# Input loads moved from ACT's DMA queue into SP's queue, between the output stores, in a batched q·kᵀ kernel on Trainium2

## Chip, cores, metric

One core of one Trainium2 chip. The metric is the device time of one execution in microseconds (us), lower is better. A run is called slow when it is over 1.5% above the fastest of the same kernel, and fast otherwise. The profile is one execution, and all profile times count from the start of its span. It calls TensorE's matmuls PE and its weight loads PEld, VectorE DVE, ScalarE ACT, GpSimd POOL and SyncE SP. The granted clock is the share of TensorE's full clock that the profile records as allowed. A transfer lands when the profile has all of it as arrived.

## The reference

```python
# q, k: float32 [8, 12, 1024, 64]
np.einsum('bhid,bhjd->bhij', q, k).astype(np.float32)   # [8, 12, 1024, 1024]
```

Each of the 96 heads reads 0.5 MB and writes 4.19 MB. In all, 50 MB are read and 403 MB written.

## The kernel before

Heads are worked on in blocks: sizes G = 1, 1, 2, then 4, and a block has 2·G heads. I number heads from 0 throughout: blocks 0 and 1 hold heads 0 to 3, block 2 heads 4 to 7, block 3 heads 8 to 15, and so on by eights. A block's input comes in four loads (q and k of its first G heads, then q and k of its second G heads), goes through a float32 buffer (three of them; blocks 0 to 2 use the space of the first output buffer instead), is cast to float16 on POOL (GpSimd), transposed on PE during the first heads of the block before, and then multiplied. Four output buffers of 4 MB each are filled by ACT and DVE from PSUM and stored by SP.

```python
    in_pool = ctx.enter_context(tc.tile_pool(name="in_pool", bufs=3))
    half_pool = ctx.enter_context(tc.tile_pool(name="half_pool", bufs=1))
    out_pool = ctx.enter_context(tc.tile_pool(name="out_pool", bufs=4))
    ...
        def scores(self, n, side):            # one head
            ...
            for t in range(NT):               # 8 row tiles
                ...two matmuls, one copy to o_sb on DVE or ACT...
                if t in side:
                    side[t]()                 # transposes for the next block, after t = 1 and t = 6
            pin(nc.sync.dma_start(out=of[self.first + n]..., in_=o_sb...))
    ...
    def refill(i):                            # b: block i, c: block i + 1
        if b:
            ...
            for n in range(3):
                b.cast(n)
        yield
        if b:
            b.load(3, nc.scalar)
            b.cast(3)
        if c:
            c.load(0, nc.scalar)
            c.load(1, nc.scalar)
        yield
        yield
        if c:
            c.load(2, nc.scalar)
    ...
            b.scores(n, side)
            for job in todo:
                next(job, None)
            if nxt and n == nxt.G - 1 and i > 0:
                todo.append(refill(i + 2))
                next(todo[-1])
                if n == 2 * b.G - 1:
                    next(todo[-1])
```

So a refill spreads its four loads over several heads, and a load can only be issued once the cast of the piece that had its buffer is done.

Of the kernel before, what the change touches and what calls it, by code (L numbers as in the profile page):

```python
# [15 lines left out]
def kernel(  # L16
# [6 lines left out]
    nc = tc.nc  # L23
# [141 lines left out]



    def refill(i):
        b = blocks[i] if i < len(blocks) else None
        c = blocks[i + 1] if i + 1 < len(blocks) else None  # L170
        if b:
            half_sb = half_pool.tile([P, 2 * half_elems], F16, tag="half")
            b.place(half_sb, 0)
            for n in range(3):
                b.cast(n)
        yield
        if b:
            b.load(3, nc.scalar)
            b.cast(3)
        if c:  # L180
            c.load(0, nc.scalar)
            c.load(1, nc.scalar)
        yield
        yield
        if c:
            c.load(2, nc.scalar)

    blocks[0].alloc()
    for x in range(2):
# [1 line left out]
    todo = []  # L191
    for i, b in enumerate(blocks):
        nxt = blocks[i + 1] if i + 1 < len(blocks) else None
        if nxt:
            nxt.alloc()
        for n in range(2 * b.G):
            side = {}
            if nxt and n < nxt.G:
                side = {
                    1: lambda: nxt.transpose(n, 0),  # L200
                    6: lambda: nxt.transpose(n, 1),
# [4 lines that stand above are left out]
            if nxt and n == nxt.G - 1 and i > 0:  # L206
                todo.append(refill(i + 2))
                next(todo[-1])
                if n == 2 * b.G - 1:
                    next(todo[-1])  # L210


# [28 lines left out]
```

## Time and profile before

| | before |
|---|---|
| time, median of 3 | 1070.81 us (1069.8 to 1071.56) |
| bytes moved by DMA | 453.40 MB, 424 GB/s over the span |
| busy share of the span | PE 70%, DVE 47%, ACT 45%, POOL 9% |
| chain that ended last | 70% stores, 12% matmuls, 5% loads |

In the page's slices a DMA digit of 9 means that the 16 DMA engines were at least 90% busy. When every slice but the last has a 9, no compute engine sets the time, whatever its own share. The prediction shows these lines and reads them.

### The profile page before, as it was taken

How to read it: one execution, taken by the hardware profiler on the slowest of the kernel's cores; microseconds unless marked ns; L12 is line 12 of the kernel's file. 1: busy time of each engine (PE TensorE's matmuls, PEld its weight loads, DVE VectorE, ACT ScalarE, POOL GpSimd, SP SyncE). 2: the span in 40 equal slices, each digit the busy share in tenths (PEclk: the TensorE clock that was granted, in tenths of full speed). 3: DMA queues.
4: the chain of work that ended last, by engine and by line, in shares of the span. 5: the costliest groups of instructions: out<-in, count | busy, mean ns of one | idle time of the engine just before them, and what ended most of it. 6: DMA issues, size and time to landing. Idle time of an engine off the chain costs nothing.

```text
span 1069.1 us, 6245 instructions
## 1 busy us (share of the span) xinstructions
PE 752.0 (70%) x2304; PEld 270.0 (25%) x2304; DVE 506.9 (47%) x384; ACT 476.3 (45%) x481; POOL 91.6 (9%) x62
## 2 busy tenths in 40 slices
PE   7774976775785786677587678668668769767740
PEld 2231322321221232232122223223123223222210
DVE  4664743542652563354265356337336537433420
ACT  4442553453444444344345445435444545544530
POOL 3202020020020020002002002000100200000000
PEclk9765555555555555555555555555555555555555
DMA  9999999999999999999999999999999999999996
GB/s 391 419 407 426 433 429 433 427 429 433 429 432 430 432 432 424 437 428 432 429 429 425 431 432 430 421 436 431 424 425 434 429 432 431 432 432 433 431 431 265
DMA packets 21920, 453.40 MB, mean 424 GB/s; under 512 B 2432, under 2 KB 2432, under 8 KB 3968
## 3 DMA queue, kind: packets, MB, share of 16 engines
q1 hardware_dynamic: 14976, 406.85, 88.8%
q10 hardware_dynamic: 6912, 46.14, 10.4%
q8 instruction: 18, 0.29, 0.1%
q14 instruction: 14, 0.11, 0.0%
HBM read 50.33 MB, written 402.65 MB: 424 GB/s over the span
## 4 chain that ended last, share of the span: by engine, by line
DMA 76%; PE 15%; ACT 4%; POOL 1%; DVE 1%; issue 0%; ACTq 0%; SPq 0%; POOLq 0%
DMA out_dram<-o_sb 70%; PE ps L128 12%; ACT o_sb L132 4%; DMA x_sb<-in_k_dram 3%; DMA x_sb<-in_q_dram 2%; PE t_ps L103 2%; POOL half_sb L88 1%; DVE o_sb L130 0%; DMA early<-in_q_dram 0%; DVE qT L115 0%; DVE kT L115 0%; ACTq L132 0%; SPq L75 0%; POOLq L88 0%; SPq L136 0%
## 5 line engine op out<-in xcount | busy, mean ns | idle before, releaser
L128 PE MATMUL ps<-kT,qT 64*128 64x512 f16 x1536 | 666.5, 618 | 253.3 <-ACT o_sb L132 226.9
L132 ACT COPY o_sb<-ps 128x1024 f32<-128x1024 f32 x480 | 475.0, 1013 | 551.5 <-DMA out_dram<-o_sb 310.7
L130 DVE COPY o_sb<-ps 128x1024 f32<-128x1024 f32 x288 | 353.1, 1227 | 498.4 <-DMA out_dram<-o_sb 364.7
L128 PEld LDWEIGHTS <-qT 64*128 64x128 f16 x1536 | 196.9, 135 | 657.2 <-issue 649.8
L88 POOL CAST half_sb<-x_sb 128x2048 f16<-128x2048 f32 x44 | 82.2, 1893 | 766.7 <-PE t_ps L103 547.7
L103 PE MATMUL t_ps<-ident,half_sb 128*128 128x128 f16 x768 | 97.8, 307 | 29.3 <-POOL half_sb L88 29.3
L115 DVE COPY qT<-t_ps 128x1024 f16<-128x1024 f16 x48 | 110.6, 2304 | 13.7 <-PE t_ps L103 13.7
L103 PEld LDWEIGHTS <-half_sb 128*128 128x128 f16 x768 | 73.1, 140 | 106.5 <-issue 73.6
L115 DVE COPY kT<-t_ps 128x1024 f16<-128x1024 f16 x48 | 58.3, 1215 | 16.0 <-PE t_ps L103 16.0
L88 POOL CAST half_sb<-early 128x512 f16<-128x512 f32 (+1 forms) x12 | 8.7, 755 | 5.6 <-DMA early<-in_q_dram 5.3
L132 ACT ACT_TABLE_LOAD x1 | 1.3, 1283 | 7.8 <-DMA early<-in_q_dram 7.8
masks.py:199 POOL TENSOR_SCALAR_AFFINE_SELECT ident<-ident 128x128 f16<-128x128 f16 x1 | 0.3, 292 | 0.1
masks.py:197 POOL MEMSET ident<- 128x128 f16 x1 | 0.2, 204 | 0.3 <-POOLq L225 0.3
L225 POOL MEMSET const-float32-0.0<- 128x1 f32 x1 | 0.1, 98 | 0.2 <-issue 0.2
L225 POOL MEMSET const-bfloat16-1.0<- 128x1 bf16 x1 | 0.1, 101 | 0.0
L225 POOL MEMSET const-uint8-127<- 128x1 uint8 x1 | 0.1, 101 | 0.0
L225 POOL MEMSET const-float32-1.0<- 128x1 f32 x1 | 0.1, 98 | 0.0
## 6 DMA issues: line engine op xcount, KB each, us to landing
out_dram<-o_sb SPq DMA_DIRECT2D x96, 4096.0 KB, 34.1
x_sb<-in_k_dram ACTq DMA_DIRECT2D x22, 1024.0 KB, 18.7
x_sb<-in_q_dram ACTq DMA_DIRECT2D x20, 1024.0 KB, 29.6
x_sb<-in_q_dram SPq DMA_DIRECT2D x2, 1024.0 KB, 11.5
early<-in_q_dram SPq DMA_DIRECT2D x4, 256.0 KB, 5.0
early<-in_k_dram ACTq DMA_DIRECT2D x4, 256.0 KB, 5.2
early<-in_q_dram SPq DMA_DIRECT2D x2, 512.0 KB, 7.4
early<-in_k_dram ACTq DMA_DIRECT2D x2, 512.0 KB, 8.0
```

What stands on the lines that cost most here:

```text
L88: nc.gpsimd.tensor_copy(out=self.halves[n % 2][:, :, n // 2], in_=self.raw[n].rearrange("p (r d) -> p r d", d=D),)
L103: pin(nc.tensor.transpose(t_ps[:, t], rows, ident))
L115: pin(nc.vector.tensor_copy(out=dst, in_=src))
L128: pin(nc.tensor.matmul(ps[:, js], qT[cs, g, t], kT[cs, g, js]))
L130: pin(nc.vector.tensor_copy(out=o_sb[:, t], in_=ps))
L132: pin(nc.scalar.copy(out=o_sb[:, t], in_=ps))
L225: nc = _bacc.Bacc("TRN2", target_bir_lowering=False, num_devices=1)
```

## The change

Its intent: keep all later traffic on one queue, in an order that the program fixes, and take the DMA issues off ACT, which also copies results. The loads go to `nc.sync`, at slightly other places between the stores.

```diff
-        yield
-        if b:
-            b.load(3, nc.scalar)
+            b.load(3, nc.sync)
             b.cast(3)
         if c:
-            c.load(0, nc.scalar)
-            c.load(1, nc.scalar)
-        yield
+            c.load(0, nc.sync)
         yield
         if c:
-            c.load(2, nc.scalar)
+            c.load(1, nc.sync)
+        yield
+        yield
+        yield
+        if c:
+            c.load(2, nc.sync)
...
                 todo.append(refill(i + 2))
                 next(todo[-1])
-                if n == 2 * b.G - 1:
-                    next(todo[-1])
```

## The prediction

> **What bounds the kernel now.** I read the page's slices, queues and issue table first, then busy time by stretches of time, then the issue times on SP's and ACT's queues, and last the chain that ended last over its first 175 us. The page:
>
> ```profile
> DMA  9999999999999999999999999999999999999996
> GB/s 391 419 407 426 433 429 433 427 429 433 429 432 430 432 432 424 437 428 432 429 429 425 431 432 430 421 436 431 424 425 434 429 432 431 432 432 433 431 431 265
> ...
> q1 hardware_dynamic: 14976, 406.85, 88.8%
> q10 hardware_dynamic: 6912, 46.14, 10.4%
> ...
> out_dram<-o_sb SPq DMA_DIRECT2D x96, 4096.0 KB, 34.1
> x_sb<-in_k_dram ACTq DMA_DIRECT2D x22, 1024.0 KB, 18.7
> x_sb<-in_q_dram ACTq DMA_DIRECT2D x20, 1024.0 KB, 29.6
> ```
>
> The DMA engines are full from the first slice to the last but one, and SP's queue (q1) alone takes 88.8% of them. PE is busy 70% of the span and no other engine over 47%. So bytes bound the kernel: 453.40 MB at 430 GB/s are 1054 us of the 1069.1 us span, and the rest is start and end. The stretches say what loads beside stores cost (columns: stretch, its length, busy us of PE, PEld, DVE, ACT, POOL, granted clock, DMA share, GB/s):
>
> ```profile
> 58.10:63.20 5.10, 3.11 (x14) 1.49 (x14) 1.22 (x1) 1.07 (x2) 1.89 (x1) 0.50 0.94 386
> 63.20:70.00 6.80, 6.80 (x28) 2.86 (x26) 5.61 (x4) 3.79 (x4) 0.00 (x0) 0.50 1.00 366
> 85.60:107.50 21.90, 10.38 (x36) 4.00 (x36) 7.42 (x6) 4.99 (x6) 4.70 (x3) 0.50 1.01 432
> 110.00:862.00 752.00, 547.30 (x1657) 195.89 (x1656) 367.49 (x276) 341.00 (x344) 65.32 (x35) 0.50 1.00 430
> 882.00:1042.00 160.00, 115.39 (x306) 38.87 (x305) 71.71 (x56) 79.14 (x80) 0.00 (x0) 0.50 1.00 432
> ```
>
> From 110 to 862 us loads run beside stores at 430 GB/s; from 882 to 1042 us there are stores only, at 432. There is nothing to win in the steady part but 0.5%. What can move the time is an interval in which the DMA engines have nothing queued. Only the start comes near that; its chain:
>
> ```profile
> 41.53 16.56 DMA x_sb<-in_k_dram
> 58.09 0.05 issue
> 58.14 1.90 POOL half_sb L88
> 60.05 0.05 issue
> 60.09 1.03 PE t_ps L103 x8
> ...
> 84.71 17.71 DMA x_sb<-in_k_dram
> 102.42 0.05 issue
> 102.47 1.90 POOL half_sb L88
> 104.38 0.05 issue
> 104.42 1.03 PE t_ps L103 x8
> ```
>
> Twice PE waits for the cast of a late load, finishes the head with it, and SP issues that head's store at 63.16 and 107.50 us: 5.07 and 5.08 us after the load landed. While PE waited, the queue lived on earlier stores.
>
> **What the Trainium skill says.** Page "DMA: Bandwidth & Descriptors", section "Where 436 GB/s comes from", puts the ceiling of the 16 ports at 435.2 GB/s; the store-only stretch at 432 agrees. (The same section has HBM's side bind at about 358; this trace does not show that.) Section "Issuing engines are not separate DMA queues" says that DMAs from any issuer run on the same 16 engines and interleave, so that a second issuer saves only issue time; 430 against 432 agrees. Section "Queues, rings and completion order" says that an engine takes turns between queues packet by packet and takes one queue's descriptors in order. The trace agrees: a store row is 32 KB and a load row 8 KB (mean packets 27 and 6.7 KB), so in turns loads get about 8/40 of 430 GB/s, 12.2 us for 1 MB (estimate), and the landings at 90.3, 102.4 and 139.2 us lie 12.1 and three times 12.3 us apart. Page "DMA: Bandwidth & Descriptors", section "Anatomy of one DMA", says that any wait on a semaphore happens on the issuing sequencer before dispatch; SP's row of waits (848.4 us of the span in front of stores) agrees.
>
> **The change part by part.** I number heads from 0. The built program keeps the order of PE, DVE and POOL; ACT loses its 41 later loads, and SP issues them between stores.
>
> Removed: 41 issues on ACT at 0.34 us, 14 us beside 45% of busy time. ACT is not the bound: zero. Also removed: the turn-taking that lets a load pass the stores in front of it.
>
> Moved: the third load of each refill (the q piece of the second half) is now issued after the fourth further store, one head later in the steady part, where it used to go after the third. In the one short block (heads 4 to 7) it moves from behind head 5 (71.17 us before) to behind head 7.
>
> Added: a load waits on SP for its raw buffer, that is for a cast, and the stores behind it wait too.
>
> Steady part. A store takes 4.19 MB / 430 = 9.75 us, a load 2.44 us, so a block of eight stores and four loads takes 87.8 us. A head is made in about 7 us without transposes (16 matmuls x 0.43 us) and 9 us with them. Four output buffers let about three stores wait behind the one that runs; the median landing of 34.1 us says 3.5 stores. The waits of SP in front of loads are two or three casts of 1.89 us after the transposes, some 2 to 6 us, against a cushion of at least three stores less the making of one head, 29 - 9 = 20 us. A load issued behind a store lands within some 35 us, and its cast is needed four or more heads later. So nothing runs dry: zero per block, eleven blocks.
>
> First gap, head 4. The k load that head 4's second transpose needs is issued at 41.5 us, as before, but directly behind store 3 (issued 41.52). By 41.5 us 24.1 MB were issued (7.34 of loads, four stores) and 403 x 41.5 = 16.7 MB moved, so 7.4 MB or 17.2 us are left; the load lands at about 41.5 + 17.2 + 2.4 = 61.1, plus up to 1 us, against 58.1. Store 4 comes 5.07 us after that, at about 66.5. Behind the load only one more load is queued, 2.44 us. Issue to first byte is about 1.3 us (first issue at 0.74 us, first bytes at about 2). The gap is 5.07 - 2.44 + 1.3 = 3.9 us. The kernel before lost something here too: from 41.5 to 70 us it moved about 1.0 MB less than at 432, 2.3 us. If that goes away, the net is +1.6; if not, +3.9. I take +2.5.
>
> Second gap, head 8. Its first transposes (after row tile 1) need the third load of the block, now issued behind store 7. Heads 5 to 7 follow store 4 by 22.4 us (63.16 to 85.58 before), so that store 7 and the load are issued at about 89. Everything older runs first: from about 68 us four stores and one load, 41.4 us, then it, landing at about 112 instead of 90.3. PE stands still until its cast is done, 1.94 us later. From there the trace before has 92.22 to 97.7 for transposes and row tiles 2 to 6 (5.5 us), and then 3.1 us from the second transposes to the store's issue: together 10.5 us from landing to store 8. Meanwhile the queue holds only two loads, 4.9 us. The gap is 10.5 - 4.9 + 1.3 = 6.9 us, and some 0.4 us for the load's landing after its last byte: 7.3 us. It does not depend on when the load lands. Before, the DMA engines lost nothing here (432 GB/s from 85.6 to 107.5).
>
> After it. Stores 9 to 11 follow at 9 to 10.3 us, transposes included, against 9.75 us a store plus one load between: margins of about 3 us, tight but dry nowhere. From head 12 on 7 us a head fill the queue again.
>
> Sum: 1070.8 + 2.5 + 7.3 = 1080.6. Every idle microsecond of the bound adds to the end, as nothing later catches up with it. I say **1080.5 us**, 0.9% longer.
>
> **The rivals.**
> - The loads are hidden anyway (same time, 1071): the bytes are the same, and the early waits might be covered by the backlog. For it: 430 GB/s at every place after 110 us. Against: the backlog behind the late load, 4.9 us, is shorter than the 10.5 us that the next store needs.
> - One queue is served better (1064 to 1068): without turn-taking the engines don't switch between 32 KB stores and 8 KB loads. For it: a queue's time per MB, 10.4% x 1069.1 / 46.14 = 2.41 us for loads against 2.33 for stores, and 366 to 386 GB/s near 60 us. Against: 3% of 46 MB are 3 us at most, and the early small loads explain part. Even 435 GB/s throughout would save only some 12 us, so faster by over 2% (21 us) is out of reach.
> - Waits at SP's head empty the queue in every block (1100 and more): 3 us in eleven blocks would be 33 us. For it: a load's buffer waits for a cast that waits for another load in the same queue. Against: that older load is then behind at most one or two stores, and one more store stands behind it. I find the cushion of 15 to 20 us hard to use up, but this is the only way to slower by over 2%.
>
> **Range and chances.** The second gap is firm within 2 us, the first within 3; the turn-taking may give back up to 3, and a third gap at heads 9 to 11 may add up to 4. That makes 1074 to 1088. Faster 0.01, same 0.93, slower 0.06.
>
> **What would show it.** Right: SP's queue alone carries about 450 MB; loads land later than the 18.7 and 29.6 us of before, in the thirties; throughput falls well below 400 GB/s near 64 us and near 120 us, and is 430 from 160 us on; store 8 is issued about 10.5 us after the late q load landed, at about 122; the shift of late stores against before is the sum of the two gaps and then constant. Wrong: stores shifted by less than 4 us at 200 us; or a shift that grows from block to block (the third rival); or a steady rate that differs from 430 by more than 2 GB/s.

## The result

The changed kernel takes **1090.26 us** (median of 4, 1087.41 to 1090.55) against 1071.18 us (median of 4, 1069.80 to 1072.11) for the kernel before. The ratio is 1.0173, 95% interval 1.0153 to 1.0194. Ratios here are the mean time of one kernel's fast runs over that of the other's of the same rounds, so not quite the ratio of the medians. It is inside 2%, but 19 us longer where the prediction had 10, and outside its range of 1074 to 1088.

The page of the changed kernel: the slices, the stores' queue, and the issues with their median time to landing (last column, us).

```profile
DMA  9989799999999999999999999999999999999994
GB/s 385 423 316 424 302 394 422 439 430 423 430 433 424 432 432 427 429 425 434 424 429 435 429 433 430 425 438 428 428 434 428 435 427 437 429 436 430 437 427 212
...
q1 hardware_dynamic: 20880, 449.85, 96.8%
...
out_dram<-o_sb SPq DMA_DIRECT2D x96, 4096.0 KB, 34.3
x_sb<-in_q_dram SPq DMA_DIRECT2D x22, 1024.0 KB, 37.5
x_sb<-in_k_dram SPq DMA_DIRECT2D x21, 1024.0 KB, 36.0
```

Slices 3 and 5 (54 to 82 us and 109 to 136 us) have fallen to 316 and 302 GB/s; a full engine set gives 430. From slice 7 on the row looks like the one of before. The loads now land after some 36 to 38 us instead of 19 to 30. The same in stretches, first the kernel before and then the changed one (columns as in the prediction; the last two are DMA share and GB/s):

```profile
41.50:70.00 28.50, 16.78 (x62) 6.70 (x60) 12.95 (x9) 8.81 (x9) 5.57 (x3) 0.50 0.99 397
110.00:140.00 30.00, 29.76 (x100) 11.17 (x99) 23.10 (x17) 17.68 (x19) 4.45 (x3) 0.50 1.01 431
```

```profile
41.50:70.00 28.50, 11.16 (x38) 3.96 (x35) 8.30 (x6) 6.31 (x7) 7.15 (x4) 1.00 0.81 335
110.00:140.00 30.00, 19.20 (x73) 7.99 (x74) 14.07 (x10) 9.73 (x10) 3.79 (x2) 1.00 0.71 292
200.00:880.00 680.00, 485.93 (x1474) 173.81 (x1473) 326.43 (x246) 302.98 (x306) 57.88 (x31) 1.00 1.00 430
```

From 200 to 880 us both kernels move 430 GB/s, and from 880 to 1040 us both 432. So the loss is made before 200 us. In time at 430 GB/s it is (397 - 335) x 28.5 / 430 = 4.1 us in the first stretch, (431 - 292) x 30 / 430 = 9.7 us in the second, and by the same working 1.8 us from 70 to 110 us (430 against 411 GB/s) and 1.2 us from 140 to 200 us (432 against 423): 16.8 us. The spans differ by 1088.8 - 1069.1 = 19.7 us; the other 3 us lie after 1040 us, where the queue drains. The chain of the changed kernel names the waits:

```profile
43.52 21.09 DMA x_sb<-in_k_dram
64.61 0.05 issue
64.67 1.91 POOL half_sb L88
...
96.64 21.90 DMA x_sb<-in_q_dram
118.55 0.05 issue
```

The first is the load that head 4 needs, issued right behind store 3; the second is the load that head 8 needs, issued right behind store 7. The timeline has the stores that depend on them at 69.69 us (5.08 after the landing) and 128.97 us (10.42 after it). Before, the same stores were issued at 63.16 and 107.50 us. The second gap in steps of 2 us:

```profile
122.00:124.00 2.00, 2.00 (x6) 0.66 (x5) 2.00 (x1) 1.41 (x2) 0.98 (x1) 1.00 0.03 12
124.00:126.00 2.00, 2.00 (x7) 0.55 (x6) 1.29 (x2) 1.37 (x2) 0.00 (x0) 1.00 0.00 0
```

PE and DVE are busy with head 8, and the DMA engines have nothing at all to move. The engines do not stop together: from 120 to 122 us the share is still 0.60, and a share of 0.03 of 16 engines over the next 2 us is one engine for 1 us. So the last of the sixteen stops 1 to 2 us after most of the others.

### The profile page after: what moved, and what is told of

Its sections match the earlier page's. It is cut to its first block, busy times and chain, and to the rows that moved or that the text cites. A ratio compares the mean times of both kernels' runs of the same rounds, so it can differ in the third digit from the quotient of the medians.

```text
span 1088.8 us, 6260 instructions
## 1 busy us (share of the span) xinstructions
PE 759.5 (70%) x2304; PEld 272.4 (25%) x2304; DVE 507.7 (47%) x384; ACT 476.5 (44%) x481; POOL 91.8 (8%) x62
## 4 chain that ended last, share of the span: by engine, by line
DMA 71%; PE 20%; ACT 5%; POOL 0%; issue 0%; DVE 0%; SPq 0%; ACTq 0%
DMA out_dram<-o_sb 67%; PE ps L128 17%; ACT o_sb L132 5%; PE t_ps L103 3%; DMA x_sb<-in_q_dram 2%; DMA x_sb<-in_k_dram 2%; DMA early<-in_q_dram 0%; POOL half_sb L88 0%; DVE o_sb L130 0%; DVE kT L115 0%; ACTq L132 0%; SPq L136 0%; SPq L75 0%
```

## The experiments

**Theory A:** the loss comes from two places in the start, where a load that a head needs now waits behind stores on the same queue, and the stores in front run out before that head's own store can be issued. **Rival B:** one queue costs something in every block, by SP being held in front of a load or by a worse order of transfers. **Rival C:** the later place of the third load is the cause, whatever the queue. Times of the kernel before in the same jobs were 1070.5 to 1071.0 us (medians).

### e1_start_on_act and e2_start_on_sp: which refills matter

```diff
+    def refill_old(i): ...      # as in the kernel before
-                todo.append(refill(i + 2))
+                old = i + 2 < 5         # e1;  e2: i + 2 >= 5
+                todo.append((refill_old if old else refill)(i + 2))
                 next(todo[-1])
+                if old and n == 2 * b.G - 1:
+                    next(todo[-1])
```

> The changed kernel, but the first two refills (loads issued up to head 11) as in the kernel before, on ACT's queue and at the old places; the other nine on SP at the new places. Theory A (the loss lies in gaps at heads 4 and 8, where loads wait behind stores; nothing in the steady part): as the kernel before, 1070 to 1074 us, no stretch below 350 GB/s after 50 us. Rival B (one queue costs something in every block: SP held at its head by a load, or stores and loads in one order are served worse): nine elevenths of the loss stay, 1083 to 1088 us.

> The reverse: only the first two refills are changed (SP, new places), the other nine as before on ACT. Theory A: all of the loss, 1087 to 1091 us, with gaps near 68 and 126 us. Rival B: two elevenths of it, 1073 to 1076 us.

Measured: e1 1071.58 us (ratio 1.0004, 0.9988 to 1.0021), e2 1087.51 us (1.0155, 1.0140 to 1.0170). The first two of eleven refills carry the loss; the other nine, on SP, leave the time where it was, within some 2 us by the interval. That agrees with A. Against the changed kernel e2 lacks some 3 us; see r1 and r2.

### e3_place_only and e4_queue_only: the two halves of the change

```diff
     # e3: the changed kernel's refill, on ACT
-            b.load(3, nc.sync)          (and the three others)
+            b.load(3, nc.scalar)
     # e4: the kernel before, on SP
-            b.load(3, nc.scalar)        (and the three others)
+            b.load(3, nc.sync)
```

> Half of the change: the loads keep the new places in program order, but on ACT's queue. Theory A with the queue as the cause: a load passes the stores, about 12 us per 1 MB, so the load issued behind head 7 lands at about 100 us instead of 118 and the store queue hardly runs dry: 1070 to 1076 us. Rival C (the later place of the third load alone is the cause): near the changed kernel, 1082 to 1090 us.

> The other half: the loads keep the old places in program order but are issued on SP's queue. Theory A: the loads of the start still wait behind stores, but the third load is ahead of heads 6 and 7 and one more load lies behind the gating ones, so both gaps shrink to some 3 us each: 1075 to 1081 us. Rival C: as the kernel before, 1070 to 1073 us. Rival B: near the changed kernel, 1086 to 1090 us.

Measured: e3 1077.90 us (1.0065), e4 1080.97 us (1.0094). Neither half is free and neither is the whole. For e3 my number was too low: with the new places, even on ACT, the third load of the block lands at 107.2 us and the fourth, which head 8 then waits for, at 115.5, and the DMA share from 110 to 135 us is 0.82, so 4.5 us are idle. For e4 the shares are 0.82 of 15 us and 0.87 of 25 us, 2.7 and 3.3 us idle, as A had it. Rival C falls in its pure form: the place costs 7 us and the queue 10 us, each by itself, and together 19 to 20. The idle time is the larger part of each, not the whole (4.5 of 7 and 6.0 of 10 us).

### f2_one_load_on_act and f3_two_loads_on_act: one gap at a time

```diff
     # f2: one load of 41
-            b.load(3, nc.sync)
+            b.load(3, nc.scalar if i == 3 else nc.sync)
     # f3: two loads of 41
-            b.load(3, nc.sync)
+            b.load(3, nc.scalar if i == 4 else nc.sync)
     ...and the third load of that block behind head 5 on ACT, where it was before
```

> The changed kernel with one of its 41 moved loads back on ACT's queue: the k load that head 4 waits for. Theory A: it lands at about 60 instead of 64.6 us, store 4 is issued at about 65.5 instead of 69.7, the idle time near 68 us falls from 5 to about 1 us; the gap near 126 us stays. 1083 to 1087 us against some 1090 for the changed kernel. Rival B (a cost in every block): within 1 us of the changed kernel.

> The changed kernel with two loads put back, the two that head 8 waits for: the third of the block behind head 5 on ACT, as before, and the fourth on ACT. Theory A: the gap near 126 us (8.4 us without any packet) goes, the one near 68 us stays: 1078 to 1082 us. Rival B: within 1 us of the changed kernel.

Measured: f2 1085.49 us (1.0140), f3 1078.48 us (1.0071). The two gaps in stretches; the changed kernel, f2, f3:

```profile
60.00:75.00 15.00, 8.38 (x31) 3.58 (x32) 5.78 (x4) 4.00 (x5) 1.90 (x1) 1.00 0.68 282
110.00:135.00 25.00, 14.45 (x52) 5.78 (x53) 10.81 (x8) 7.66 (x8) 3.79 (x2) 1.00 0.67 287
```

```profile
60.00:75.00 15.00, 14.76 (x62) 6.32 (x63) 11.44 (x8) 8.37 (x9) 0.00 (x0) 0.57 0.95 397
110.00:135.00 25.00, 19.54 (x74) 8.05 (x75) 14.41 (x11) 9.73 (x10) 3.79 (x2) 0.50 0.63 248
```

```profile
60.00:75.00 15.00, 8.54 (x32) 3.57 (x32) 5.95 (x4) 4.16 (x5) 1.89 (x1) 0.50 0.67 279
110.00:135.00 25.00, 20.36 (x76) 8.49 (x77) 15.45 (x11) 10.09 (x11) 1.89 (x1) 0.50 1.03 440
```

One minus the share, times the length, is the idle time: 4.8 and 8.3 us in the changed kernel; 0.8 and 9.3 in f2; 5.0 and none in f3. Each gap goes with its own loads (one in f2, two in f3, one of which also went back to its old place) and leaves the other about as it was, so three loads out of 41 decide. Rival B had expected no change from them. Against some 1090.5 us for the changed kernel f2 saves 5 us and f3 12, more than the idle time that went (4.0 and 8.3): the slow stretch behind a gap, told of under m1, goes with the gap. From 79 to 84 us f2 moves 449 GB/s, and f3, which keeps the first gap, 270.

### h1_loads_ahead_of_store: the same one queue without the gaps

```diff
-            b.scores(n, side)
+            b.scores(n, side, ahead)   # 'ahead' starts the refill just before the store of this head
...
         yield
+        if c and i <= 4:
+            c.load(2, nc.sync)         # two heads earlier, first two refills only
         yield
         yield
-        if c:
+        if c and i > 4:
             c.load(2, nc.sync)
```

> All moved loads stay on SP's one queue, but the first two of each refill are issued ahead of the store of their head instead of behind it, and the third load of the first two refills is issued two heads earlier. Theory A: the gating loads land some 10 us earlier, with a whole store queued behind them, so neither gap opens; 1068 to 1073 us on one queue, level with the kernel before or a little faster. Rival B (one queue is the cost): 1085 us or more.

Measured: 1071.94 us (5 rounds), ratio 1.0010, 0.9996 to 1.0023. The stretches and one row of SP's waits (total us, times, longest):

```profile
60.00:75.00 15.00, 15.00 (x60) 6.27 (x60) 13.11 (x10) 8.36 (x9) 0.00 (x0) 1.00 1.00 430
110.00:135.00 25.00, 24.75 (x87) 9.34 (x85) 19.07 (x13) 14.01 (x15) 0.00 (x0) 1.00 1.00 429
```

```profile
SPq L75 <- POOL half_sb L88: 115.2, 21, 9.6
```

All loads are on SP, no gap is left, and the time is that of the kernel before. The head-of-queue part of rival B falls most clearly here: SP stood in front of loads for 115 us in all, waiting for casts, with the stores held behind them, and it cost nothing because the DMA engines had older stores to move meanwhile (from 200 to 880 us their share is 1.00, at 430 GB/s). In the changed kernel that wait is 5.9 us.

### m1_second_load_later: the slow stretches

In the changed kernel there are stretches in which the engines are busy but move far less than 430 GB/s.

```diff
         yield
-        if c:
+        if c and i > 4:
             c.load(1, nc.sync)
         yield
+        if c and i <= 4:
+            c.load(1, nc.sync)
```

> Only about the slow stretches: in the changed kernel the engines are busy but move 156 to 262 GB/s from 79 to 84 us and 258 to 262 from 138 to 142, where a lone load lies behind the first store after a gap. Here those two loads (the second of the first two refills) go behind the next head's store instead. If a load in the seam behind a store that started on all engines at once is slow, each stretch moves one store later or goes, and up to 3 us are saved: 1087 to 1090 us. If the stretch belongs to the store's own end, it stays at 79 and 138 us and the time stays as it was.

Measured: 1090.86 us (1.0186). The changed kernel, its repeat r1 (see below), then m1:

```profile
79.00:84.00 5.00, 5.00 (x18) 1.74 (x16) 4.50 (x4) 3.50 (x4) 0.00 (x0) 1.00 1.02 272
88.00:93.00 5.00, 5.00 (x18) 1.87 (x16) 4.74 (x3) 2.54 (x3) 0.00 (x0) 1.00 1.05 452
```

```profile
79.00:84.00 5.00, 5.00 (x18) 1.88 (x17) 4.51 (x4) 3.19 (x4) 0.00 (x0) 1.00 0.69 184
```

```profile
79.00:84.00 5.00, 4.44 (x23) 1.95 (x22) 5.00 (x5) 3.19 (x4) 0.00 (x0) 0.82 0.98 419
88.00:93.00 5.00, 5.00 (x19) 1.89 (x18) 4.50 (x4) 2.94 (x3) 0.34 (x1) 0.50 0.92 247
```

The stretch follows the load to its new place behind store 5: 247 GB/s from 88 to 93 us, at a share of 0.92. The other one, 138 to 143 us with 261 GB/s, rises to 419 and comes back, weaker, at 147 to 152 us (324 against 423). So it belongs to the load between two stores, not to the store's own end. Moving it saves nothing. What one costs is known roughly: (430 - 272) x 5 / 430 = 1.8 us here, and 2.9 us by r1, the same kernel again. The view books a packet wholly where it starts (from 71 us on it gives 524, 0 and 524 GB/s in steps of 1 us), so rate and share of 5 us scatter. In h1, where a load follows store 4 too but older stores are still queued ahead of it, 60 to 75 us runs at 430. What the engines wait for in such a stretch stays open.

### r1_changed_again, r2_start_on_sp_again, h2_start_ahead_rest_act: the rest, and a try at beating both

r1 is the changed kernel and r2 is e2, both unaltered. h2 takes h1's first two refills and the kernel before's nine others:

```diff
-            if nxt and n == nxt.G - 1 and i > 0:
+            if nxt and n == nxt.G - 1 and i in (1, 2):
                 fresh.append(refill(i + 2))
...
+            if nxt and n == nxt.G - 1 and i > 2:
+                todo.append(refill_old(i + 2))
+                next(todo[-1])
```

> The changed kernel unaltered, on the same chip as the next run. 1088 to 1091 us; the idle stretches at 68 and 126 us as before. It tells whether the 2.8 us by which it differed from the kernel with only the first two refills changed are real.

> Only the first two refills changed, again. If the steady part on SP costs nothing (theory A in full): within 1 us of the changed kernel in this same job. If the nine later refills on SP cost something (a small rest of rival B): 2 to 3 us less than the changed kernel, again.

> A try at beating both: the first two refills on SP with their loads ahead of the stores (no gap), the later nine on ACT as in the kernel before. Theory A: nothing idle, so again at the bytes' limit: 1069 to 1072 us, not distinguishable from the kernel before.

Measured: r1 1090.54 us (1089.33 to 1091.17), r2 1087.23 us (1086.93 to 1088.48), h2 1071.44 us (ratio 1.0011, 0.9999 to 1.0024). The 3.3 us between r1 and r2 come after the gaps and are real, as the ranges do not touch (of the changed kernel's eight runs in all, one, at 1087.41, lies among r2's): a small rest of rival B. Both kernels have the same shares in the gaps (0.67 and 0.67) and from 200 to 1040 us the same rate (430 and then 432 GB/s); they differ in the drain after it, where r1 takes 47.5 us for 14.9 MB and r2 45.1 us for as much. In the medians the same exchange of the nine refills is worth nothing clear when the start has no gaps (e1 against before 1.0004; h1 1071.94 against h2 1071.44). The profiles show the longer drain there too: e1 31.4 us for 7.7 MB, the kernel before 29.1 us for 8.2; h1 30.9 us for 7.9 MB, h2 29.6 us for 8.0. But the profiled executions of e1 and h1 were the slowest of their kernels' four and five runs, so whether the rest needs the gaps stays open, and so does its cause. h2 doesn't beat the kernel before, and no run did: what it could save, the idle DMA time, is nil already.

## Why the prediction was wrong in size and right in part of the mechanism

- **What bounds the kernel**: right. The steady part is 430 GB/s in both, the loss is idle DMA time, and a shift made in the start is never caught up.
- **The two gaps**: right in place and cause; e2, f2, f3 and h1 show it. Head 4's store follows its load by 5.08 us (predicted 5.07), head 8's by 10.42 (predicted 10.5).
- **The step that counts what is still to move when the load lands** failed in size, in both gaps: "only one more load is queued, 2.44 us", and "only two loads, 4.9 us" less 0.4 us for the landing (which the first gap's sum left out). A load lands when the slowest of 16 engines has done its part, and by then the others were well into the loads behind it. The engines as a whole stopped at about 65.4 us, 0.8 us after the landing at 64.61, and at about 121.2 us, 2.7 us after the landing at 118.55. The 1.3 us from issue to first byte was 0.8 in both gaps (69.69 to 70.5 us, 128.97 to 129.8 us), which takes part of this back. So the gaps are 4.8 and 8.3 us, not 3.9 and 7.3.
- **The step "If that goes away, the net is +1.6; if not, +3.9. I take +2.5"** failed: the loss that the kernel before has there did not go away. From 41.5 to 70 us the changed kernel is 6.4 us short of 432 GB/s, and only some 4.5 us of that are the gap. Net, the first stretch costs 4.1 us.
- **The step "tight but dry nowhere" after head 8** counted queued bytes at 430 GB/s. Nothing ran dry, but a load between stores that had just started went slowly (272 and 261 GB/s in the two stretches). That is, by stretches and with the rest of the first gap in it, 1.8 us from 70 to 110, 1.4 us (9.7 less the gap's 8.3) from 110 to 140 and 1.2 us from 140 to 200: 4.4 us with no term in the sum.
- **The end of the queue** had no term either: 3 us, as r1 and r2 show.
- The sum measured is 4.1 + 8.3 + 4.4 + 3 = 19.8 us, against 2.5 + 7.3 = 9.8. Of the error of 10 us about a quarter (1.6 + 1.0) is terms too small, and three quarters (4.4 + 3) are terms that were missing. Of **"the turn-taking may give back up to 3"** in the range nothing came: the steady rate is 430 GB/s in both.
- **Two of its signs** failed. Store 8 was expected at about 122 us and was issued at 128.97, because store 7 went out at 96.21 us and not at about 89; the gap does not depend on that, as the prediction said. The shift of late stores was to be constant, and a growing one was to speak for the third rival. Against before, store 20 is issued 13.6 us later, store 40 13.5, store 60 18.8, store 80 20.1 and store 95 20.2. But the bytes do not fall further behind from 200 to 1040 us (430 and 432 GB/s in both), so it is the order of loads and stores that differs there, and stores alone were a poor clock.
- **The rivals**: "hidden anyway" fell; "one queue is served better" fell (its 3 us are 3.7 by the two figures beside it; none came); "waits at SP's head empty the queue in every block" fell, by e1 and by h1's 115 us of harmless waits.

## What to carry to other kernels

When DMA bounds a kernel, ask of every load not how many bytes it moves but what stands in front of it in its queue and how much stands behind it: the time from its landing to the next store must be covered by work that is already queued. A second queue is worth having for the few loads that a head is about to wait for, because it lets them pass the stores; on one queue the same is had by issuing them ahead of the store. Look at the start, where the queue is short: three of 41 loads made the two gaps.

## What the Trainium skill lacked or had wrong

- "DMA: Bandwidth & Descriptors", section "Issuing engines are not separate DMA queues", says that a second issuer saves only issue time. For total bytes that holds (430 GB/s either way). The section leaves out what the turns between queues, told in another section that the prediction names, mean for the order. The three loads that heads 4 and 8 wait for landed 16.6, 19.1 and 17.7 us after their issue on ACT; on SP behind the stores, and issued later by 2, 25 and 12 us, they took 21.1, 21.9 and 23.9 us, and that opened 13 us of idle time.
- The same page, section "Where 436 GB/s comes from", has the HBM side (about 358 GB/s) bind transfers between HBM and SBUF. Here one core alone stores at 432 GB/s, near the section's port ceiling of 435.2. The section itself notes a load measured at 425.
- No page that I read says how far the 16 engines drift apart. Here the last one stopped 1 to 2 us after most others at 122 us, and in the last 10 us of the changed kernel the DMA share is 0.06, about one engine's worth.
- No page that I read has the slow stretch: a 1 MB load between two stores just after an idle queue, with 184 to 324 GB/s over 5 us in the changed kernel, r1 and m1.
- "TensorE: Matmul & The Clock Gate" warns that clock events in a trace can be unreliable, but has no case like this one: the mean granted TensorE clock is 0.523 in the profile of before and 1.0 in that of the changed kernel, yet ten 64x512 matmuls take 4.45 us in both, and a run of the changed kernel at 0.518 took 1090.55 us like one at 1.0.
